# A ring of weight buffers that hands out the slot used longest ago, and lets two borrowed slots in at a channel mixer's first pair

## The chip, the cores and the metric

The kernel runs on one core of a Trainium2 chip. The metric is the device time of one execution in microseconds (us), lower is better. A core has five engines with an instruction queue each, which they work through in order: PE (matrix multiplication, with its weight loads listed as PEld), DVE (vector arithmetic), ACT (activations and copies with a scale), POOL and SP. In this kernel SP does nothing but issue DMA transfers, and POOL little else.

## The reference

A decoder trunk of two layers on 256 tokens of width 2048, in fp32. Each layer has a token mixer (gated linear attention in the first, forgetting attention in the second, both with cross-attention into 256 memory tokens) and then a channel mixer. What matters here is the passage from a token mixer's output projection into the channel mixer:

```python
x = x + gla_mixer(h, mk, mv, ...)        # ends in  concatenate([o, m]) @ w_out
h = rmsnorm(x, norm_ffn[i])
x = x + conv_ffn(h, ffn_w_up[i], ffn_conv_w[i], ffn_conv_b[i], ffn_w_down[i])

def conv_ffn(h, w_up, conv_w, conv_b, w_down):
    u = causal_dwconv(h @ w_up, conv_w, conv_b)      # 2048 -> 11264, causal convolution of width 3
    a, val = split_cols(u, [FFN_HIDDEN, FFN_HIDDEN])
    return (jax.nn.silu(a) * val) @ w_down           # 5632 -> 2048
```

## The kernel before

**Weights.** All weight matrices lie in one DRAM array `wp`, cut into units of 128 partitions x up to 1024 fp32 numbers (512 KB). Each unit is loaded by SP into a slot of a ring, the tile `raw`. Because fp32 products are made from two rounded parts, ACT copies the slot into `whi` (rounded), and DVE subtracts that copy from the slot into `wlo`. Each has five buffers. PE then multiplies activations that are split in the same way: whi with both activation parts, wlo with one, so that an ordinary unit of the projections shown here is 12 matmuls of 128x128 by 128x512. A slot is free again when its subtraction is done, a pair of whi and wlo buffers when PE is done with them. `split_unit` (load L232, copy L242, subtraction L243) does this for one unit.

**The ring.** Five slots lie in a tile of their own, `home`. During a channel mixer two more are added, halves of a tile `guest` (named raw2) that is allocated in a pool of that time. `raw_slot()` picks the slot of each load: a counter modulo the present length of the list. `ffn` appends the two guests when it begins and cuts the list back to five at its end.

**Pairs.** Most units of the mixers are worked by `pair_steps`. It takes a plan of the units of one panel; some neighbouring two of them form a pair, which is computed with seven block products (21 matmuls) in place of eight, by a scheme of Strassen's kind. Such a pair loads its two units at once (L440, into `ra` and `rb`), makes two copies and subtractions from them (`split_more`: L391, L392), then four subtractions in place (L446 to L449), and two further copies and subtractions. The first panel of a mixer is units 0 to 5 singly, then the pair (6, 7), then units 8 to 15. Its first pair multiplies sums of token blocks too (`usum`, made at L1460, L485 to L488, L696, L697).

**Into the channel mixer.** The output projection (`add_out`, its last panel at L347) produces 4 blocks of 512 columns. Each is added to x (L507), transposed by DVE into a tile `blk` (L1637), sent to DRAM (`far<-blk`, L659, on SP's queue), and later brought back turned (L664) and scaled and split into the activations' two parts (L551, L553). The returns of the last two blocks belong to the mixer's first panel: they are issued after units 2 and 9 and split after units 3 and 11. The tile `guest` is allocated once the pool that held `blk` has been closed, so its memory, and that of `usum`, can be that of `blk`.

**Order.** A scheduler orders the instructions of each engine's queue from the written order, priorities and its own estimate of times. Loads, copies and subtractions of weights have a priority 300 places ahead of where they are written. `tc.issue_after(i)` puts an instruction behind i on the same engine. The scheduler also adds every wait: the load into a slot waits for the last reader of that slot, or of what lay in that memory before.

Queues that matter: SP issues the unit loads, the transfers of the projection's blocks and the returns of blocks in the mixers' first panels; POOL issues the transfers inside the mixers.

Of the kernel before, what the change touches and what calls it, by code (L numbers as in the profile page):

```python
# [39 lines left out]
RAWS = 5  # L40
# [5 lines left out]
NUNIT = 1024  # L46
# [102 lines left out]
def _trunk(ctx: ExitStack, tc: tile.TileContext, xt, xtok, memt, wp, wgu, gns, gfin, cnv, par, msk, out):  # L149
# [36 lines left out]

    loads, casts, lows, ends, last_mm, sent = [], [], [], [], [], []
    home = rear.tile([P, RAWS * NUNIT], F32, name="raw")
    slots, taken = [home[:, i * NUNIT : (i + 1) * NUNIT] for i in range(RAWS)], [0]

    def raw_slot():

        taken[0] += 1
        return slots[taken[0] % len(slots)]
    scratch = [sm]
    parked = []

# [2 lines left out]
    def work(tag, bufs=1):  # L200
        return pwork.tile([P, 512], F32, name="ps_" + tag, tag=tag, bufs=bufs)
# [17 lines left out]
    def split_unit(unit, pieces=1, before=None, between=int):  # L219

        off, kcs, n = unit
        w = len(kcs) * n
        with tc.high_priority(offset=AHEAD):
            raw = raw_slot()
            hi = wpool.tile([P, NUNIT], F32R, name="whi", tag="whi", bufs=5)
            lo = wpool.tile([P, NUNIT], F32R, name="wlo", tag="wlo", bufs=5)
            src = wp[off : off + P * w].rearrange("(p n) -> p n", p=P)
            for i in range(pieces):
                s = slice(i * w // pieces, (i + 1) * w // pieces)
                if i:  # L230
                    between()
                loads.append(nc.sync.dma_start(raw[:, s], src[:, s]))  # L232
            if n % P:
                a, b, c = (t.rearrange("p (j m) -> p j m", j=len(kcs))[:, :, :n] for t in (raw[:, :w], hi, lo))
                casts.append(S.activation(b, a, AF.Copy))
                lows.append(V.tensor_tensor(c, a, b.bitcast(F32), ALU.subtract))
                return hi, lo
            for i in range(pieces):
                s = slice(i * w // pieces, (i + 1) * w // pieces)
                if before is not None:  # L240
                    before(i)
                casts.append(S.activation(hi[:, s], raw[:, s], AF.Copy))  # L242
                lows.append(V.tensor_tensor(lo[:, s], raw[:, s], hi[:, s].bitcast(F32), ALU.subtract))  # L243
        return hi, lo
# [141 lines left out]
    def split_more(src, n):  # L386

        with tc.high_priority(offset=AHEAD):
            hi = wpool.tile([P, NUNIT], F32R, name="whi", tag="whi", bufs=5)
            lo = wpool.tile([P, NUNIT], F32R, name="wlo", tag="wlo", bufs=5)  # L390
            casts.append(S.activation(hi[:, :n], src, AF.Copy))  # L391
            lows.append(V.tensor_tensor(lo[:, :n], src, hi[:, :n].bitcast(F32), ALU.subtract))  # L392
        return hi, lo

    def pair_steps(units, src, sums, flip, pool, early, late, ahead=0):

        bank = {}
        fast, slow = ("p1", "p5", "p7", "p6"), ("p2", "p3", "p4", "x")
        accs, works = (slow, fast) if flip else (fast, slow)
        tags = {n: ("acc", 4) for n in accs}  # L400
        tags.update(zip(works, (("o", 1), ("s", 2), ("s", 2), ("t", 1))))
        begun = set()
        sums = dict(sums)
        n = len(units)
        single = [k for k in range(n) if k not in sums and k - 1 not in sums]
        plan = []
        at = 0
        while at < n:
            if at + ahead in sums:
                plan.append(at + ahead)  # L410
                at += 2
            else:
                plan.append(single.pop(0))
                at += 1
        end = [k for k in plan if k in sums]

        def mm(name, x, w, last):
            if name not in bank:
                tag, bufs = tags[name]
                bank[name] = (pacc.tile([P, 512], F32, name="acc", tag="acc") if tag == "acc" else work(tag, bufs))  # L420
            r = TE.matmul(bank[name], x, w, start=name not in begun, stop=last)  # L421
            begun.add(name)
            return r

        def tok(k, b):
            return [src[k][:, part, b * P : (b + 1) * P] for part in range(2)]

        def three(name, x, w, last=False):
            for i, (a, b) in enumerate(((0, 0), (1, 0), (0, 1))):
                r = mm(name, x[a], w[b], last and i == 2)  # L430
            return r

        places = (("p2", 0, 0), ("p4", 1, 0), ("p3", 0, 1), ("x", 1, 1))
        for k in plan:
            if k in sums:
                with tc.high_priority(offset=AHEAD):
                    ra, rb = raw_slot(), raw_slot()
                    with tc.issue_after(loads[-1].ins):
                        for t, (off, _, w) in ((ra, units[k]), (rb, units[k + 1])):
                            loads.append(nc.sync.dma_start(t, wp[off : off + P * w].rearrange("(p n) -> p n", p=P)))  # L440
                st = [[sums[k][:, part, j, :] for part in range(2)] for j in (3, 0, 1, 2)]
                done = k == end[-1]
                w1 = split_more(ra[:, :512], 512)
                w2 = split_more(rb, 1024)
                with tc.high_priority(offset=AHEAD):
                    V.tensor_tensor(ra[:, :512], ra[:, 512:], ra[:, :512], ALU.subtract)  # L446
                    V.tensor_tensor(ra[:, 512:], rb[:, 512:], ra[:, 512:], ALU.subtract)  # L447
                    V.tensor_tensor(rb[:, 512:], rb[:, 512:], ra[:, :512], ALU.subtract)
                    summed = V.tensor_tensor(rb[:, :512], rb[:, :512], rb[:, 512:], ALU.subtract)  # L449
                three("p1", tok(k, 0), [t[:, :512] for t in w1], done)  # L450
                three("p2", tok(k + 1, 0), [t[:, :512] for t in w2])
                three("p3", st[3], [t[:, 512:] for t in w2])
                with tc.issue_after(summed.ins):
                    w3 = split_more(ra, 1024)
                three("p5", st[0], [t[:, :512] for t in w3], done)
                three("p7", st[2], [t[:, 512:] for t in w3], done)
                w4 = split_more(rb, 1024)
                three("p6", st[1], [t[:, 512:] for t in w4], done)
                last_mm.append(three("p4", tok(k + 1, 1), [t[:, :512] for t in w4]))
                if done:  # L460
                    with tc.issue_after(casts[-1].ins), tc.issue_after(lows[-1].ins):
                        early(bank)
                yield -1
                yield -1
                continue
            else:
                w = split_unit(units[k])
                last = k == n - 1
                steps = [(low, *place) for low in range(2) for place in places]
                if last:  # L470
                    steps.sort(key=lambda t: places.index(t[1:]))
                for low, name, b, h in steps:
                    for part in range(2 - low):
                        r = mm(name, tok(k, b)[part], w[low][:, h * 512 : (h + 1) * 512], last and low == 1)
                    if last and low:
                        ends.append(r)
                        late(b, h, bank[name])
                last_mm.append(r)
            yield k
# [923 lines left out]
    def ffn(l, nx, h, m, ys, zs, landing, then, pool, temps, last=None, spare=None):  # L1403
        with tc.tile_pool(name=f"ffn{l}", bufs=1) as fp:
# [3 lines left out]
            up_sums = {k: held("usum", k) for k in (*SEVEN_UP, SEVEN_MORE)}  # L1408
            rooms = {i: held("dsum", i) for i in range(2)}
            guest = pool.tile([P, 2 * NUNIT], F32, name="raw2")  # L1410
            slots.extend(guest[:, i * NUNIT : (i + 1) * NUNIT] for i in range(2))
            cw = fp.tile([P, 4 * 88], F32, name="cw")
            nc.sync.dma_start(cw, cnv[l])
            taps = [fp.tile([P, 2, 2, T + i], F32, name=f"tap{i}") for i in range(3)]
# [181 lines left out]
            else:  # L1596
                hooks = {(2, 3): then.land, (2, 5): then.land, (2, 7): then.take, (3, 1): then.take, (3, 2): then.land,
                         (3, 5): then.take}
                for f, step, at in ((2, f2, 3), (3, f3, 0)):
                    for u in range(at, 8):  # L1600
                        step(u)
                        hooks.get((f, u), int)()
            del slots[RAWS:]

    def preparing(name, dst, pool, far, kept=None, tag="blk", queue=nc.sync):

# [72 lines left out]
    with tc.tile_pool(name="store", bufs=1) as op:  # L1679
# [58 lines left out]
        then.begin, then.rooms = begin, None  # L1738
        more = [op.tile([P, 2, T], F32R, name=f"more{i}") for i in range(RING - KC)]
        ffn(1, n, bufA, bufB + more, ys, zs, zs, then, op, temps, last, spare)  # L1740


# [68 lines left out]
```

## Time and profile before

| | |
|---|---|
| time, median of 3 runs | 2221.41 us (2220.82 to 2221.58) |
| profiled execution, its own time | 2219.84 us |
| its span | 2218.0 us |
| busy: PE, PEld, DVE, ACT, POOL | 2196.9, 1846.7, 1828.6, 1437.8, 136.8 us |
| mean granted clock of PE | 0.997 |
| unit loads | 811 issues (741 of 512 KB, 70 smaller) |
| HBM read, written | 469.62 MB, 43.79 MB |

A row of a timeline has the start and the length in us, the engine, the line of the code, the operation, what it writes and reads, and how many instructions are merged in it; in brackets stands how long the engine had been idle and what ended that. A row of waits has who waited, for whom, the total in us, how many times, and the longest. A row of a table by stage has the stage, its length, the busy time (and number of instructions) of PE, PEld, DVE, ACT and POOL, the granted clock of PE, the share of the DMA engines and GB/s. Matmul lengths in a timeline overlap; the pace of PE is read from the starts. The first channel mixer begins at about 456 us of the span, the second at about 1493 us.

### The profile page before, as it was taken

What the parts mean: (1) busy time and instruction counts of PE and PEld (TensorE: products, weight loads), DVE (VectorE), ACT (ScalarE), POOL (GpSimd) and SP (SyncE); (2) the same over time, 40 slices, a digit from 0 to 9 for tenths busy, and PEclk for the clock granted to TensorE, in tenths of its full rate; (3) what the DMA queues carried; (4) which work ended last, traced back from release to release, by engine and by line L of the source; (5) the groups of instructions that cost most, each with busy time, mean ns of one, the idle gap of its engine ahead of it and who ended that gap; (6) DMA issues with size and microseconds to landing.
All of it is one profiled execution on the core that took longest, in us unless ns stands there. A gap on an engine that the chain in (4) does not pass through costs nothing.

```text
span 2218.0 us, 30190 instructions
## 1 busy us (share of the span) xinstructions
PE 2196.9 (99%) x10285; PEld 1846.7 (83%) x10285; DVE 1828.6 (82%) x2715; ACT 1437.8 (65%) x2280; POOL 136.8 (6%) x257
## 2 busy tenths in 40 slices
PE   9999999999999999999999999999999999999998
PEld 7888888878888888888888998877888888888886
DVE  7768976679988889889987569668998888988996
ACT  6655655557887568647865555445788657765874
POOL 0000000001100000001010000000100000100000
PEclk9999999999999999999999999999999999999999
DMA  9766666776777667666877667666687667776683
GB/s 360 260 222 217 199 207 230 252 231 223 258 250 239 199 228 256 231 207 224 268 246 245 219 207 235 224 217 223 224 263 248 222 203 245 242 236 211 230 283 113
DMA packets 166291, 515.41 MB, mean 232 GB/s; under 512 B 20780, under 2 KB 42552, under 8 KB 166136
## 3 DMA queue, kind: packets, MB, share of 16 engines
q1 hardware_dynamic: 149064, 460.99, 63.2%
q0 software_dynamic: 16496, 51.71, 7.4%
q8 instruction: 80, 1.31, 0.2%
q10 hardware_dynamic: 576, 0.79, 0.1%
q14 instruction: 75, 0.61, 0.1%
HBM read 469.62 MB, written 43.79 MB: 231 GB/s over the span
## 4 chain that ended last, share of the span: by engine, by line
PE 96%; DVE 2%; ACT 1%; DMA 1%; issue 0%; SPq 0%; DVEq 0%; ACTq 0%
PE acc L421 29%; PE acc L347 26%; PE ps_s L421 15%; PE ps_o L421 7%; PE ps_t L421 7%; PE acc L273 3%; PE acc L318 3%; PE ps_s L347 2%; PE acc L377 2%; PE acc L271 1%; PE ps_s L1044 0%; DMA raw<-wp 0%; ACT whi L242 0%; PE ps_o L710 0%; PE ps_s L710 0%
## 5 line engine op out<-in xcount | busy, mean ns | idle before, releaser
L243 DVE TENSOR_TENSOR wlo<-raw,whi 128x1024 fp32r<-128x1024 f32 (+2 forms) x685 | 812.5, 1200 | 222.9 <-ACT whi L242 200.8
L242 ACT ACTIVATE whi<-raw 128x1024 fp32r<-128x1024 f32 (+2 forms) x685 | 704.3, 1045 | 347.8 <-PE acc L347 131.2
L347 PE MATMUL acc<-whi,B 128*128 128x512 f32 (+3 forms) x1248 | 290.9, 369 | 0.0
L391 ACT ACTIVATE whi<-raw 128x1024 fp32r<-128x1024 f32 (+1 forms) x184 | 173.7, 953 | 179.4 <-DVE raw L447 65.7
L347 PEld LDWEIGHTS acc<-whi,B 128*128 128x128 f32 x1248 | 226.8, 188 | 28.1
L392 DVE TENSOR_TENSOR wlo<-raw,whi 128x1024 fp32r<-128x1024 f32 (+1 forms) x184 | 198.3, 1084 | 26.8 <-ACT whi L391 23.8
L421 PE MATMUL acc<-whi,mix 128*128 128x512 f32 x746 | 191.7, 392 | 8.7 <-ACT whi L242 8.7
L421 PE MATMUL acc<-whi,B 128*128 128x512 f32 x720 | 186.9, 389 | 0.0
L421 PEld LDWEIGHTS acc<-whi,mix 128*128 128x128 f32 x746 | 141.2, 189 | 38.7 <-ACT whi L242 9.2
L347 PE MATMUL acc<-wlo,B 128*128 128x512 f32 (+3 forms) x624 | 159.1, 369 | 0.0
L421 PEld LDWEIGHTS acc<-whi,B 128*128 128x128 f32 x720 | 135.1, 188 | 28.5 <-ACT whi L242 0.5
L347 PEld LDWEIGHTS acc<-wlo,B 128*128 128x128 f32 x624 | 114.2, 188 | 14.6
L1425 ACT ACTIVATE tap<-yzu,cw 128x256 f32<-128x256 f32 x264 | 120.7, 534 | 5.4 <-DMA yzu<-far 5.4
L1425 ACT ACTIVATE tap<-fvt,cw 128x256 f32<-128x256 f32 x264 | 120.2, 530 | 3.1 <-DMA fvt<-far 3.1
L1432 DVE TENSOR_TENSOR tap<-tap,tap 128x1024 f32<-128x1024 f32 x88 | 106.7, 1213 | 9.0 <-ACT tap L1425 9.0
L421 PE MATMUL acc<-wlo,mix 128*128 128x512 f32 x373 | 105.0, 392 | 0.0
L421 PE MATMUL acc<-wlo,B 128*128 128x512 f32 x360 | 103.8, 389 | 0.0
L421 PE MATMUL ps_s<-whi,mix 128*128 128x512 f32 x374 | 103.8, 389 | 0.0
L421 PE MATMUL ps_s<-whi,B 128*128 128x512 f32 x324 | 89.9, 389 | 0.0
L421 PEld LDWEIGHTS acc<-wlo,mix 128*128 128x128 f32 x373 | 70.6, 189 | 14.8
L421 PEld LDWEIGHTS ps_s<-whi,mix 128*128 128x128 f32 x374 | 70.2, 188 | 14.6
L421 PEld LDWEIGHTS acc<-wlo,B 128*128 128x128 f32 x360 | 67.6, 188 | 14.0
(503 smaller groups left out, 3912.8 us busy)
## 6 DMA issues: line engine op xcount, KB each, us to landing
raw<-wp SPq DMA_DIRECT2D x741, 512.0 KB, 4.6
fvt<-far POOLq DMA_DIRECT2D x100, 128.0 KB, 5.2
raw<-wp SPq DMA_DIRECT2D x32, 384.0 KB, 3.4
far<-yu POOLq DMA_DIRECT2D x22, 512.0 KB, 3.0
far<-yzu POOLq DMA_DIRECT2D x22, 512.0 KB, 3.0
yzu<-far POOLq DMA_DIRECT2D x88, 128.0 KB, 4.8
raw<-wp SPq DMA_DIRECT2D x24, 388.0 KB, 3.5
x<-xtok SPq DMA_DIRECT2D x8, 512.0 KB, 7.0
```

Source lines behind the costliest of these rows:

```text
L242: casts.append(S.activation(hi[:, s], raw[:, s], AF.Copy))
L243: lows.append(V.tensor_tensor(lo[:, s], raw[:, s], hi[:, s].bitcast(F32), ALU.subtract))
L271: mm = TE.matmul(acc[p][c][:, :T], w[:, s], both[:, 0, :], start=False, stop=end and j == 3)
L273: mm = TE.matmul(acc[p][c], w[:, s], both, start=u == j == 0, stop=end and j == 3)
L318: mm = TE.matmul(acc[b][:, :n], src[kcs[j] - base][:, part, b * P : (b + 1) * P], w, start=u == 0 and low == part == j == 0, stop=u == end ...
L347: mm = TE.matmul(acc[b][:, :n], src[kc - base][:, part, b * P : (b + 1) * P], ready[low][:, j * room : j * room + n], start=i == low == pa ...
L377: mm = TE.matmul(acc[b][:, :n], src[kc - base][:, part, b * P : (b + 1) * P], w, start=i == low == part == j == 0, stop=i == end and low = ...
L391: casts.append(S.activation(hi[:, :n], src, AF.Copy))
L392: lows.append(V.tensor_tensor(lo[:, :n], src, hi[:, :n].bitcast(F32), ALU.subtract))
L421: r = TE.matmul(bank[name], x, w, start=name not in begun, stop=last)
L1425: S.activation(by_run(taps[i][:, s, c, i:]), zs[slot][:, :, 2 * c + s], AF.Copy if i else AF.Identity, bias=0.0 if i else w[3], scale=w[2 ...
L1432: V.tensor_tensor(taps[0], taps[0], taps[n][:, :, :, :T], ALU.add)
```

## The change

`raw_slot` now rotates the list: the slot at the front, the one handed out longest ago, goes to the back and is handed out. `ffn` no longer appends its two guests at once; it keeps them in `coming`, and the next `pair_steps` pair puts them at the front of the list just before it takes its two slots. At the end of `ffn` the guests are filtered out of the list wherever they stand.

```diff
-    slots, taken = [home[:, i * NUNIT : (i + 1) * NUNIT] for i in range(RAWS)], [0]
+    slots, coming = [home[:, i * NUNIT : (i + 1) * NUNIT] for i in range(RAWS)], []
 
     def raw_slot():
 
-        taken[0] += 1
-        return slots[taken[0] % len(slots)]
+        slots.append(slots.pop(0))
+        return slots[-1]
...
             if k in sums:
                 with tc.high_priority(offset=AHEAD):
+                    slots[:0] = coming
+                    del coming[:]
                     ra, rb = raw_slot(), raw_slot()
...
             guest = pool.tile([P, 2 * NUNIT], F32, name="raw2")
-            slots.extend(guest[:, i * NUNIT : (i + 1) * NUNIT] for i in range(2))
+            guests = [guest[:, i * NUNIT : (i + 1) * NUNIT] for i in range(2)]
+            coming.extend(guests)
...
-            del slots[RAWS:]
+            slots[:] = [s for s in slots if not any(s is g for g in guests)]
```

## Prediction

> **What bounds the kernel now.** First the page: span, the chain that ended last, then who made PE wait.
>
> ```profile
> span 2218.0 us, 30190 instructions
> ...
> PE 96%; DVE 2%; ACT 1%; DMA 1%; issue 0%; SPq 0%; DVEq 0%; ACTq 0%
> ```
>
> ```profile
> PE acc L421 <- ACT whi L242: 8.7, 1, 8.7
> PE ps_o L185 <- DVE B L182: 1.5, 1, 1.5
> PE ps_t L421 <- ACT whi L391: 0.9, 1, 0.9
> ```
>
> PE carries 96% of the chain, so a change pays only where it shortens a PE stall. The waits of PE name one large stall, 8.7 us, and two small ones; the 1.5 us is the start of the program. PE's timeline puts the large one at the first unit of the second channel mixer (L421 is its matmul, L347 that of the output projection ahead of it):
>
> ```profile
> 1488.06 1.98 PE L347 MATMUL acc<-whi,B 128*128 128x512 f32 x8
> 1489.87 1.07 PE L347 MATMUL acc<-wlo,B 128*128 128x512 f32 x4
> ...
> 1493.04 0.61 PE L347 MATMUL acc<-wlo,B 128*128 128x512 f32 x2
> 1502.39 3.78 PE L421 MATMUL acc<-whi,mix 128*128 128x512 f32 x8 [8.73 <-ACT whi L242]
> ...
> 1510.46 1.75 PE L421 MATMUL acc<-whi,mix 128*128 128x512 f32 x7
> ```
>
> Eight matmuls start 1489.87 - 1488.06 = 1.81 us apart: 0.2268 us each, the undisturbed rate, 2.72 us for a unit of 12. The last two of the projection start at 1493.04, so the next could start at 1493.49; it starts at 1502.39, 8.90 us late. The 24 matmuls of units 0 and 1 then take 1510.46 - 1502.39 = 8.07 us and not 24 x 0.2268 = 5.44: 2.63 us more. The table by stage says why:
>
> ```profile
> 1498.00:1502.00 4.00, 0.00 (x0) 0.00 (x0) 0.69 (x1) 1.18 (x2) 0.00 (x0) 0.50 0.74 261
> 1502.35:1510.40 8.05, 8.01 (x24) 6.38 (x25) 8.03 (x14) 6.97 (x10) 0.00 (x0) 0.67 0.65 196
> 1510.40:1520.00 9.60, 9.60 (x44) 7.93 (x44) 7.81 (x10) 3.18 (x3) 0.00 (x0) 1.00 0.89 247
> ```
>
> The granted clock (third column from the end) falls to 0.50 in the idle stretch, is 0.67 over the two units and 1.00 after them. The stall costs 8.90 + 2.63 = 11.53 us. What it waited for is in the chain of that window:
>
> ```profile
> 1495.16 2.57 DMA far<-blk
> ...
> 1497.78 3.42 DMA raw<-wp
> ...
> 1501.28 1.06 ACT whi L242
> ```
>
> The load of unit 0 could not be issued until the normalised input's last block (blk) had been read out to DRAM: the slot it goes to is a guest slot, and its memory was blk's.
>
> **The ring, by counting calls.** From the loops of the code, 160 slots are taken before the first mixer, 264 in it, 120 between the mixers, 264 in the second. The old rule takes the counter modulo the length, so at a change of length it jumps. First mixer: unit 0 gets the slot of the load just before it; units 1 to 4 the slots of six loads before; unit 5 guest a, unit 6 guest b, unit 7 slot 0. Second mixer: unit 0 gets guest b; units 1 to 5 the slots of six before; unit 6 guest a, unit 7 guest b again. The new rule gives units 0 to 5 slots used five loads before, and units 6 and 7, the first pair, the two guests. From the pair on the distance is seven under both, and after the first mixer five (seven for one load). So only the first eight loads of each mixer differ; all loads, copies and matmuls remain in number and size.
>
> **Second mixer, units 0 to 5.** The release of a slot is the end of the subtraction (wlo, L243) that last read it:
>
> ```profile
> 1469.41 1.22 DVE L243 TENSOR_TENSOR wlo<-raw,whi 128x1024 fp32r<-128x1024 f32 x1 [1.50 <-ACT whi L242]
> 1470.66 0.35 SPq L232 DMA_DIRECT2D raw<-wp  x1
> ...
> 1482.39 0.85 SPq L232 DMA_DIRECT2D raw<-wp  x2
> 1495.16 0.33 SPq L659 DMA_DIRECT2D far<-blk  x1
> 1497.78 0.33 SPq L232 DMA_DIRECT2D raw<-wp  x1
> 1498.16 0.42 SPq L440 DMA_DIRECT2D raw<-wp  x1
> 1493.12 0.42 ACT L635 ACTIVATE sq<-x 128x256 f32<-128x256 f32 x1 [11.27 <-DVE x L507]
> ```
>
> The slot of five loads before unit 0 (unit 3 of the projection's last panel) is free at 1469.41 + 1.22 = 1470.63; before, unit 1's load took it at 1470.66. Now unit 0 goes there, 27 us earlier than 1497.78, and units 1 to 4 take the places of units 2 to 5, the last by 1482.39 + 0.85. They were landing that early already, but ACT, which works in order, sat idle 11.27 us behind unit 0's copy. That copy can now run at about 1482, when the projection's unit 3 gives back its whi buffer, against a need at 1493.49. Unit 5 reuses unit 0's slot and is needed five units later. This removes 11.53 us.
>
> **The first pair is late next.** Both its loads wait for blk's transfer (before, the one at L440, 1498.16, did, and the other waited for unit 0's guest). Behind them on SP's queue may stand units 8 to 11 and the return of the last block (L664); ACT's copy of usum shares the same memory. When blk leaves here is not in the trace, since PE stood still. The nearest rows are the first mixer's, where PE ran through:
>
> ```profile
> 456.60:482.10 25.50, 24.55 (x106) 19.48 (x106) 17.21 (x27) 12.75 (x22) 0.00 (x0) 1.00 0.70 217
> ```
>
> ```profile
> 456.66 1.07 PE L421 MATMUL acc<-whi,B 128*128 128x512 f32 x4
> ...
> 477.50 0.73 PE L421 MATMUL ps_t<-whi,usum 128*128 128x512 f32 x2 [0.92 <-ACT whi L391]
> ...
> 482.16 1.98 PE L421 MATMUL acc<-whi,B 128*128 128x512 f32 x8
> ```
>
> ```profile
> 461.23 0.33 SPq L659 DMA_DIRECT2D far<-blk  x1
> 465.97 0.33 SPq L232 DMA_DIRECT2D raw<-wp  x1
> 466.35 0.90 SPq L440 DMA_DIRECT2D raw<-wp  x2
> ```
>
> ```profile
> 469.33 1.06 ACT L242 ACTIVATE whi<-raw 128x1024 fp32r<-128x1024 f32 x1 [2.65 <-DMA raw<-wp]
> 470.69 0.63 ACT L391 ACTIVATE whi<-raw 128x512 fp32r<-128x512 f32 x1 [0.30 <-DMA raw<-wp]
> 472.46 1.07 ACT L391 ACTIVATE whi<-raw 128x1024 fp32r<-128x1024 f32 x1 [1.13 <-DMA raw<-wp]
> ...
> 476.38 1.06 ACT L391 ACTIVATE whi<-raw 128x1024 fp32r<-128x1024 f32 x1 [1.52 <-DVE raw L449]
> ```
>
> There blk left 461.23 - 456.66 = 4.57 us after unit 0 began and was away 465.97 - 461.23 = 4.74 us later; then three guest-bound loads (unit 5, unit 6, unit 7) landed at about 469.33, 470.69, 472.46. With unit 5 out of the queue the pair lands one place earlier: 469.33 and 470.69. From unit 7's landing to the end of the pair's last copy took 476.38 + 1.06 - 472.46 = 4.98 us, so that copy would end at 475.67. PE, unhindered, has 72 matmuls of units 0 to 5 and 15 of the pair ahead of its use: 456.66 + 87 x 0.2268 = 476.39. Slack 0.7 us. In the second mixer the same offsets from 1493.49 give the same 0.7 us: hidden, barely. I bound the pair's new stall per mixer between 0 and the 1.69 us that the first mixer loses now (next), and take 0.15 us each, since the computed slack is positive but smaller than a landing varies.
>
> The blk transfer took 2.57 us in the idle machine at 1495.16 and 4.74 us at 461.23 amid loads; I used the longer. The Trainium skill, "DMA: Bandwidth & Descriptors", section "Latency and other measured facts", says the receipt of a write to HBM is slower under load; the two rows agree in direction.
>
> **First mixer.** The 106 matmuls of that window include one already running, so 105 started between 456.66 and 482.16: 25.50 us against 105 x 0.2268 = 23.81, a loss of 1.69 us, 0.92 of it at the pair's last operand. Now unit 5 has an ordinary slot (unit 0's, read by about 448) and the pair lands earlier, as above. It gains 1.69 at most and, with the copies in the same order and the same late release, 0 at least. Unit 0's load also stops waiting for the load just before it; that hit no PE wait, so it counts nothing.
>
> **Sum.** 11.53 + 1.69 - 2 x 0.15 = 12.9 us. Elsewhere PE has no wait to lose or win; the return to five slots costs nothing, as that load is only looser. The profiled execution's own time is 2219.84 us (span 2218.0), 1.57 below the median 2221.41: 2221.41 - 12.9 = 2208.5.
>
> On the clock: the Trainium skill, "TensorE: Matmul & The Clock Gate", Part 1, gives half clock after an idle window of about 3.4 us, lifted after about 3.4 us of work. Half a rate lost over 3.4 us would be an estimate of 1.7 us for my 2.63, and 2209.4 in all; the trace has the low clock longer, so the rows stand.
>
> **Rivals.** (a) The pair takes over the wait. For: slack of 0.7 us in a chain of transpose, transfer, load, two copies and four subtractions. Against: the same chain met the first mixer's pace nearly. If blk leaves 2 us later (SP's in-order queue holding one more load, that of unit 12, ahead of it), each mixer's pair stalls about 1.3 us: 2208.2 + 2.6 = 2210.8. With 3 us each, 2214. (b) The first mixer gains nothing: 2221.41 - 11.53 + 0.15 = 2210.0. (c) Within 0.2% (4.4 us, about what this kernel's measurement can tell): the order is computed anew by the scheduler, and if it again puts a guest-bound item, such as ACT's usum copy, ahead of unit 0's copy, PE stalls as before: about 2221. For: in the second mixer usum's copy did stand ahead of it. Against: in the first it stands behind unit 4's. (d) Slower: the pair in the second mixer waits so long that more than the 11.53 us comes back. Its place is SP's queue at the guest loads; it decides when they issue over 13 us later than 1493.49 + 9.31 = 1502.8, past 1516, and 4.4 us more to be told, that is past 1520. Only a load that waits for late work, put ahead of blk's transfer, could do that; the longest candidates I see are 2 us.
>
> **Chances.** Forecast, 2206 to 2210: 0.62. (a) and (b), up to 2214: 0.24. Between that and (c): 0.05. (c) 0.05. (d) 0.04. Faster 0.90, within 0.2% 0.06, slower 0.04. The range is 2206 (the full 13.2 us and 2 us of run-to-run) to 2213.
>
> **What would show it.** In the second mixer: PE without a wait at the first unit, clock 1.00 through it, the unit loads at L232 before blk's far transfer, both loads at L440 right after it. In the first: L440's two loads follow blk's transfer with no L232 between, and ps_t's 0.92 us gone. The prediction is wrong if a PE wait of over 2 us appears at a first pair, or if waits appear far from both places.

## The result, and the profile after

The changed kernel takes 2210.43 us (median of 5 runs, 2208.67 to 2210.61) against 2221.41 us before (5 runs, 2219.92 to 2224.24): a ratio of 0.9948, 95% interval 0.9935 to 0.9962, so 11.0 us less. The profiled execution of the new kernel has its median time, 2210.43 us; the one of before stands 1.57 us under its median. Between the two profiles there are therefore only 9.4 us, and it is those that the accounts below divide up. Lines of the code after the change are 2 or 3 higher than before (L440 is L442, L659 is L661).

The head of the page and the waits of PE, after:

```profile
span 2208.6 us, 30197 instructions
...
PE 95%; DVE 2%; DMA 1%; ACT 1%; issue 0%; SPq 0%; DVEq 0%; ACTq 0%
```

```profile
PE ps_t L421 <- ACT whi L391: 2.0, 4, 1.2
PE ps_o L185 <- DVE B L182: 1.5, 1, 1.5
PE acc L347 <- ACT whi L242: 0.3, 1, 0.3
```

The 8.7 us at the second mixer's first unit are gone, and `ps_t` of the pairs has risen from 0.9 us in one wait to 2.0 us in four: 0.29 and 1.18 us at the two first pairs, and 0.23 and 0.26 us at the first pairs of the two second panels (569.88 and 1607.51 us). PE's timeline at that first unit (L347 is the projection, L421 the mixer):

```profile
1492.99 0.62 PE L347 MATMUL acc<-wlo,B 128*128 128x512 f32 x2
1493.44 1.07 PE L421 MATMUL acc<-whi,mix 128*128 128x512 f32 x4
...
1514.07 0.73 PE L421 MATMUL ps_t<-whi,usum 128*128 128x512 f32 x2 [1.18 <-ACT whi L391]
```

Unit 0 follows 0.45 us after the last two matmuls of the projection started, that is without a gap; 1.18 us are waited 20 us later, at the first pair. The table by stage (columns as before the change; the granted clock is third from the end):

```profile
1498.00:1502.00 4.00, 4.00 (x19) 3.34 (x18) 0.01 (x1) 1.06 (x1) 0.00 (x0) 1.00 0.73 242
1502.35:1510.40 8.05, 8.05 (x37) 6.69 (x36) 4.27 (x7) 2.57 (x4) 0.00 (x0) 1.00 0.75 236
1510.40:1520.00 9.60, 8.42 (x37) 6.60 (x37) 9.48 (x14) 7.75 (x12) 0.00 (x0) 1.00 0.57 164
```

Where the clock stood at 0.50 and 0.67 it is now 1.00, and the 8.05 us that held 24 matmuls hold 37. The stage after them is the one that has got worse: PE is idle for 9.60 - 8.42 = 1.18 us of it. SP's timeline there:

```profile
1480.92 16.79 SPq L232 DMA_DIRECT2D raw<-wp  x7
1498.01 0.33 SPq L661 DMA_DIRECT2D far<-blk  x1
1503.34 0.84 SPq L442 DMA_DIRECT2D raw<-wp  x2
1504.23 0.43 SPq L666 DMA_DIRECT2D yzu<-far  x1
```

The single units' loads (L232) now stand ahead of blk's transfer; the pair's two (L442) directly behind it. The chain of work that ended last, around the pair:

```profile
1497.36 0.63 DVE blk L1640
...
1498.01 5.31 DMA far<-blk
...
1503.34 0.33 SPq L442
...
1503.71 5.30 DMA raw<-wp
...
1509.10 1.07 ACT whi L391
...
1510.19 1.24 DVE wlo L392
...
1512.96 1.07 ACT whi L391
...
1514.07 0.73 PE ps_t L421 x2
```

It is the predicted chain, transfer, load, copy, subtractions, last copy, and it ends at 1512.96 + 1.07 = 1514.03, with PE waiting. In the first mixer the same chain is nearly in time; SP's timeline, and PE's:

```profile
461.27 0.33 SPq L661 DMA_DIRECT2D far<-blk  x1
466.08 0.81 SPq L442 DMA_DIRECT2D raw<-wp  x2
```

```profile
476.42 0.74 PE L421 MATMUL ps_t<-whi,usum 128*128 128x512 f32 x2 [0.29 <-ACT whi L391]
```

No load at L232 stands between the two any more, and the wait of 0.92 us there has become 0.29.

**A ledger.** Every trace has 10285 matmuls. Setting the start of the n-th of one, from the beginning of its span, against the n-th of the other shows where time is gained (negative) or lost, in us against the profile of before; "end" is the difference at the last matmul, which is that of the spans:

| kernel | first mixer, first pair | first mixer, second panel | second mixer, entry | second mixer, first pair | second mixer, second panel | elsewhere | end |
|---|---|---|---|---|---|---|---|
| after | -1.07 | +0.99 | -11.52 | +1.52 | +0.60 | 0.0 | -9.5 |
| after, repeated (e9) | -1.03 | +0.93 | -11.52 | +1.13 | +0.63 | +0.4 | -9.4 |
| e1 | +0.94 | 0 | -11.52 | +2.16 | -0.35 | +0.1 | -8.7 |
| e2 | -1.27 | +1.25 | -11.52 | +0.34 | +0.57 | +0.4 | -10.3 |
| e3 | +0.71 | 0 | -11.52 | 0 | -0.35 | +0.4 | -10.8 |
| e4 | -1.16 | +0.98 | -11.52 | 0 | -0.35 | +1.4 | -10.6 |
| e5 | -1.70 | 0 | -11.52 | 0 | -0.35 | +0.4 | -13.2 |
| e5, repeated (e11) | -1.70 | 0 | -11.52 | 0 | -0.29 | -0.6 | -14.1 |
| e6 | -0.15 | 0 | -11.52 | +1.63 | +0.49 | +1.8 | -7.8 |
| e7 | -1.70 | +0.84 | -11.52 | 0 | +1.39 | +4.8 | -6.2 |
| e8 | -1.70 | 0 | -11.52 | 0 | -0.35 | -0.3 | -13.9 |
| e10 | -1.39 | +0.24 | -11.52 | +0.03 | 0 | -0.5 | -13.2 |

The second panel is the stretch some 90 to 120 us after a mixer's beginning (about 550 to 570 and 1590 to 1616 us). Of "elsewhere", -0.6 to +0.9 us arise in the first 456 us, ahead of both mixers: profiles of single executions differ by about that much where PE's and SP's queues are the same.

### The profile page after: what moved, and what is told of

The parts are those of the page before. It is cut to its first block, busy times and chain, and to the rows that moved or that the text cites. A ratio compares the mean times of both kernels' runs of the same rounds, so it can differ in the third digit from the quotient of the medians.

```text
span 2208.6 us, 30197 instructions
## 1 busy us (share of the span) xinstructions
PE 2195.5 (99%) x10285; PEld 1845.1 (84%) x10285; DVE 1828.1 (83%) x2715; ACT 1435.6 (65%) x2280; POOL 136.8 (6%) x257
## 4 chain that ended last, share of the span: by engine, by line
PE 95%; DVE 2%; DMA 1%; ACT 1%; issue 0%; SPq 0%; DVEq 0%; ACTq 0%
PE acc L421 27%; PE acc L347 26%; PE ps_s L421 15%; PE ps_o L421 7%; PE ps_t L421 7%; PE acc L318 3%; PE acc L273 3%; PE ps_s L347 2%; PE acc L377 2%; PE acc L271 1%; ACT whi L391 0%; DMA raw<-wp 0%; DMA far<-blk 0%; DVE wlo L392 0%; PE ps_s L1046 0%
## 5 line engine op out<-in xcount | busy, mean ns | idle before, releaser
L243 DVE TENSOR_TENSOR wlo<-raw,whi 128x1024 fp32r<-128x1024 f32 (+2 forms) x685 | 815.3, 1205 | 211.7 <-ACT whi L242 194.6
L347 PE MATMUL acc<-whi,B 128*128 128x512 f32 (+3 forms) x1248 | 290.8, 369 | 0.0
L347 PEld LDWEIGHTS acc<-whi,B 128*128 128x128 f32 x1248 | 226.8, 188 | 28.1
L421 PE MATMUL acc<-whi,mix 128*128 128x512 f32 x746 | 191.3, 389 | 0.0
L421 PE MATMUL acc<-whi,B 128*128 128x512 f32 x720 | 187.4, 389 | 0.0
L421 PEld LDWEIGHTS acc<-whi,mix 128*128 128x128 f32 x746 | 140.0, 188 | 29.2
L347 PE MATMUL acc<-wlo,B 128*128 128x512 f32 (+3 forms) x624 | 159.1, 369 | 0.0
L421 PEld LDWEIGHTS acc<-whi,B 128*128 128x128 f32 x720 | 135.1, 188 | 28.3
L347 PEld LDWEIGHTS acc<-wlo,B 128*128 128x128 f32 x624 | 114.2, 188 | 14.6
L1435 DVE TENSOR_TENSOR tap<-tap,tap 128x1024 f32<-128x1024 f32 x88 | 107.1, 1217 | 14.2 <-ACT tap L1428 13.9
L421 PE MATMUL acc<-wlo,mix 128*128 128x512 f32 x373 | 105.2, 389 | 0.0
L421 PE MATMUL acc<-wlo,B 128*128 128x512 f32 x360 | 104.0, 389 | 0.0
L421 PE MATMUL ps_s<-whi,mix 128*128 128x512 f32 x374 | 103.8, 389 | 0.0
L421 PE MATMUL ps_s<-whi,B 128*128 128x512 f32 x324 | 89.9, 389 | 0.0
L421 PEld LDWEIGHTS ps_s<-whi,mix 128*128 128x128 f32 x374 | 70.2, 188 | 14.6
L421 PEld LDWEIGHTS acc<-wlo,mix 128*128 128x128 f32 x373 | 70.0, 188 | 14.5
L421 PEld LDWEIGHTS acc<-wlo,B 128*128 128x128 f32 x360 | 67.6, 188 | 14.0
```

Source lines behind the costliest of these rows:

```text
L347: mm = TE.matmul(acc[b][:, :n], src[kc - base][:, part, b * P : (b + 1) * P], ready[low][:, j * room : j * room + n], start=i == low == pa ...
L1435: V.tensor_tensor(taps[0], taps[0], taps[n][:, :, :, :T], ALU.add)
```

## Experiments

Each is an edit to the kernel after the change unless the text says before. The letters of theories are those that the expectations use: A is the account on which the prediction rests. Medians stand beside those of the kernel before that ran on the same chip.

**e1: join at the start, with the new rule.** The guests go to the back of the list when the mixer begins.

```diff
-            coming.extend(guests)
+            slots.extend(guests)
```

> The slot used longest ago is given, but the two guests are appended when the mixer begins, at the back of the ring, so that unit 5 and the first half of the pair get them in both mixers. Theory A (what costs is a guest slot used before the projection's pool is handed over, after the last block's transfer): the second mixer's 11.5 us at unit 0 are gone; the first mixer is as in the kernel before (1.7 us lost up to unit 9), and the second loses 1.5 to 3.5 us at unit 5 and the pair, since three guest-bound or later loads follow the transfer. Time 2212 to 2213. Rival B (the jump of the counter at the change of length cost, not the guests): no jump is left here, so the time is that of the changed kernel, 2210.4, and no PE wait appears at unit 5.

Measured 2211.14 us (2210.86 to 2211.48) against 2220.44, ratio 0.9958 [0.9944, 0.9973]. Its waits of PE:

```profile
PE ps_t L421 <- ACT whi L391: 2.5, 2, 1.3
...
PE acc L421 <- ACT whi L242: 0.6, 1, 0.6
```

The entry is gained whole without any late joining: five home slots go to units 0 to 4, so unit 0 gets no guest. What joining late adds is at the pair, where the ledger loses 0.94 and 2.16 us here. The total came about 1 us under theory A's and 0.7 us over its rival's. The places are A's: the 0.6 us at `acc` is unit 5 of the first mixer, where the rival had no wait. That the first mixer would be as before was a miss, since it loses 0.94 us more. The kernel after is ahead of e1 by 0.7 us by medians, or by 1.7 us if each is set against the kernel before that ran with it; it is no more than that because e1 is without the second panels' losses (ledger).

**e2: join at the first pair, with the old counter** (an edit to the kernel before).

```diff
+                    slots.extend(coming)
+                    del coming[:]
                     ra, rb = raw_slot(), raw_slot()
...
-            slots.extend(guest[:, i * NUNIT : (i + 1) * NUNIT] for i in range(2))
+            guests = [guest[:, i * NUNIT : (i + 1) * NUNIT] for i in range(2)]
+            coming.extend(guests)
```

> The old counter modulo the ring's length, with the jump at the change of length, but the guests join at the first pair. In the second mixer the pair gets both guests, as in the changed kernel; in the first mixer guest b goes to the pair's second half and guest a to unit 12. Theory A: time within 1 us of the changed kernel (2209.5 to 2211.5), the second mixer alike to 0.3 us. Rival B: the jump returns, so a good part of the 11 us does: 2215 or more.

Measured 2209.83 us (2209.25 to 2210.8) against 2220.44, ratio 0.9953 [0.9937, 0.997]. It is the kernel after, within what can be told. That the second mixer would be alike to 0.3 us was a miss: the pair loses 0.34 us here and 1.52 us after, though DVE's and SP's queues have the same order there. What differs is how long the same transfer took, 4.76 us here:

```profile
1498.42 0.33 SPq L662 DMA_DIRECT2D far<-blk  x1
1503.18 0.80 SPq L443 DMA_DIRECT2D raw<-wp  x2
```

So either half of the change by itself removes the 11.52 us, since either keeps a guest from unit 0; beside the late joining the rule of the slot used longest ago brings nothing measurable.

**e3 and e4: a tile of its own for the second mixer's guests**, in a pool opened ahead of the pool that holds `blk`; e3 is the kernel before with it, e4 the kernel after.

```diff
-            guest = pool.tile([P, 2 * NUNIT], F32, name="raw2")
+            guest = own if l else pool.tile([P, 2 * NUNIT], F32, name="raw2")
...
+    ring2 = ctx.enter_context(tc.tile_pool(name="ring2", bufs=1))
+    own = ring2.tile([P, 2 * NUNIT], F32, name="raw2")
     with tc.tile_pool(name="turn2", bufs=1) as tp:
```

> The kernel before with its counter and with guest b at unit 0 of the second mixer, but the second mixer's guests lie in a pool of their own, opened before the pool that holds the projection's blocks. Theory A: the load of unit 0 no longer waits for the last block's transfer and is issued over 20 us earlier; PE's 8.7 us wait and the low clock behind it vanish, 11.5 us in all: 2209 to 2211. The pair does not wait either. The first mixer stays as before (1.7 us lost). Rival B: the wait at unit 0 stays, 2221.

> The changed kernel with the second mixer's guests in a pool of their own, opened before the pool of the projection's blocks. Theory A: the second mixer's first pair loses the 1.3 us it has now (PE's 1.2 us wait at ps_t), the rest as the changed kernel: 2208.5 to 2209.5. A rival, that the pair's 1.3 us come from the work of the pair itself (copies and subtractions in a row on ACT and DVE, delayed by evacuations) and not from the late loads: they stay, 2210.4.

e3 measured 2209.62 us (2208.5 to 2210.72) against 2220.44, ratio 0.9952 [0.9937, 0.9966]; e4 2208.03 us (2207.99 to 2209.24), ratio 0.9946 [0.9931, 0.9961]. SP's and PE's timelines of e3, where unit 0 still takes a guest, as in the kernel before:

```profile
1481.57 1.43 SPq L232 DMA_DIRECT2D raw<-wp  x2
1483.04 3.17 SPq L440 DMA_DIRECT2D raw<-wp  x2
1488.09 10.79 SPq L232 DMA_DIRECT2D raw<-wp  x4
1499.17 0.33 SPq L659 DMA_DIRECT2D far<-blk  x1
```

```profile
1494.15 0.62 PE L347 MATMUL acc<-wlo,B 128*128 128x512 f32 x2
1494.60 1.07 PE L421 MATMUL acc<-whi,mix 128*128 128x512 f32 x4
```

All these loads, the pair's at L440 included, leave before blk does, and unit 0 follows the projection without a gap. The order of slots of before does no harm where the guest is free; the wait came from the memory alone. In e4 the 1.52 us at the second mixer's pair are gone too, which puts them down to the guests' wait for blk; its time came just below the range expected. In e3 the first mixer, whose queues on PE and SP are those of before, loses 0.71 us more than before: a pair that is late anyway varies by that much.

**e5: join one panel later.** No guest before the second panel, in both mixers.

```diff
-            coming.extend(guests)
...
                 first(k)
+            coming.extend(guests)
             done = 4
```

> The changed kernel with the guests let in one panel later: the first panel, its pair too, works on the five slots, and the guests join at the first pair of the second panel. Theory A (the pair's remaining stalls come from guest-bound loads behind the last block's transfer): the pair's loads are issued before that transfer in both mixers, PE's waits at its ps_t go (1.2 and 0.3 us; 1.3 and 0.6 us of lost pace): 2208.0 to 2209.5. Rival: seven slots are needed from the first pair on, and five make the units after it late: 2212 or more.

Measured 2206.14 us (2205.59 to 2207.08) against 2221.42, ratio 0.9932 [0.9918, 0.9946]: below the range expected. SP's timeline in the second mixer, and the stage of the first pair:

```profile
1485.65 3.05 SPq L442 DMA_DIRECT2D raw<-wp  x2
1491.09 5.36 SPq L232 DMA_DIRECT2D raw<-wp  x2
1496.74 0.33 SPq L661 DMA_DIRECT2D far<-blk  x1
```

```profile
1510.40:1520.00 9.60, 9.60 (x44) 7.97 (x43) 9.60 (x22) 7.11 (x10) 0.00 (x0) 1.00 0.89 317
```

With five slots the pair's loads leave 11 us before blk, and PE has no idle time in the stage where the kernel after has 1.18 us. The first mixer gains its 1.70 us whole. The second panels' losses are gone as well, which was not expected.

**e6: join at unit 3**, which puts a guest earlier than at the pair.

```diff
             else:
+                if k == 3:
+                    slots[:0] = coming
+                    del coming[:]
                 w = split_unit(units[k])
```

> The changed kernel with the guests let in earlier, at unit 3, so that units 3 and 4 of each mixer's first panel get them. A dose: theory A says that a guest-bound load is issued 9.4 us after unit 0 begins in the first mixer and 7 to 10 us in the second, is landed 3.4 to 5.7 us later and copied 1.06 us after that, while unit 3 is needed 8.2 us after unit 0. So PE waits 5.6 to 6 us in the first mixer and 3 to 8 us in the second, and up to 2.6 us more each where the clock falls: 2219 to 2228. Rival B (slot distances alone matter; here they are as regular as in the changed kernel): 2210.4.

Measured 2210.66 us (2209.68 to 2212.09) against 2221.42, ratio 0.9951 [0.9935, 0.9967]: a miss. SP's timeline in both mixers:

```profile
459.25 0.33 SPq L664 DMA_DIRECT2D far<-blk  x1
461.84 0.81 SPq L232 DMA_DIRECT2D raw<-wp  x2
...
1496.58 0.33 SPq L664 DMA_DIRECT2D far<-blk  x1
1499.17 0.80 SPq L232 DMA_DIRECT2D raw<-wp  x2
```

The guests' loads still wait for blk, but blk leaves 1.67 us after unit 0 (457.58 and 1494.92 here) and not 4.57, and its transfer takes 2.59 us and not 4.74 to 5.31. So the loads go out some 5 us earlier than I had reckoned in the first mixer, and unit 3 waits 0.7 us in each mixer. The offset that the prediction took from one row of before isn't a constant: in this kernel's order DVE works the split of the block ahead of blk (L558, which is L555 in the kernel after) at 467.73 us, behind blk's transposes; in the kernel after it does so in front of them.

**e7: no guests at all**, five slots throughout.

```diff
-            coming.extend(guests)
```

> The guests are allocated but never join: five slots throughout, given in turn. If the two extra slots are worth something beyond the first panel, PE waits appear at pairs or three units after them in every panel (46 pairs, 0.3 to 1 us each: 2222 to 2255). If five slots are enough for this pace (a pair's slots are free about 12 us after their loads are issued, and PE has 8 us of single units behind a pair), the time is that of the kernel with the late join, 2208 to 2212.

Measured 2213.65 us (2212.49 to 2214.71) against 2221.42, ratio 0.9966 [0.9953, 0.9979], between the two expectations. The guests are worth 2213.65 - 2206.14 = 7.5 us to e5. Nothing is lost at the first pairs. One stage late in the second mixer costs 3.51 us:

```profile
2085.00:2095.00 10.00, 10.00 (x45) 8.27 (x45) 7.09 (x11) 8.47 (x16) 0.76 (x2) 1.00 0.95 311
2095.00:2105.00 10.00, 8.42 (x29) 6.11 (x28) 9.52 (x12) 7.47 (x9) 0.00 (x0) 0.83 0.40 135
```

A pair's operand comes 1.34 us late there, the granted clock is 0.83 on average, and 29 matmuls fit where 45 did.

**e8: both cures**, late joining in the first mixer and a pool of its own in the second.

```diff
-            coming.extend(guests)
+            if l:
+                coming.extend(guests)
...
+            if not l:
+                coming.extend(guests)
             done = 4
```

> The late join (second panel) in the first mixer, and a pool of their own with the join at the first pair in the second. Theory A: no guest-bound load is late in either mixer; 2207.5 to 2209, within 1 us of the kernel with the late join in both.

Measured 2206.03 us (2205.7 to 2206.55) against 2221.42, ratio 0.9932 [0.9919, 0.9945]: below the range expected, and the same as e5. Two different ways of not waiting for blk come to the same time.

**e9 to e11, on one chip:** the kernel after once more, the kernel after with the split of the block ahead of blk asked for two units later, and e5 once more. The edit of e10:

```diff
-                {2: lambda: nx.land(landing[0]), 3: nx.take, 8: nx.col,
+                {2: lambda: nx.land(landing[0]), 5: nx.take, 8: nx.col,
```

> The changed kernel once more, for its spread and beside the next two. If the 1.3 us lost at the second mixer's first pair come of the way DMA work happens to land (the last block's transfer took 5.3 us, and the pair's second load 5.3 us), this profile shows another loss there, between 0.3 and 2 us; if they are fixed by the order of the queues, 1.2 to 1.4 us again. Time 2209 to 2211.5.

> The changed kernel, but the split of the block before the last (eight DVE operations of 0.27 us at L555, that stand in DVE's queue ahead of the last block's transposes) is written after unit 5 and not after unit 3. Theory C (the pair's loads are late because the last block reaches its transfer late, behind other DVE work): the transfer leaves 2 to 2.5 us earlier in both mixers, the pair's loads with it, and the PE waits at ps_t of the first pairs go: 1.3 and 0.6 us, 2208 to 2209. Rival D (the wait is the pair's own chain of copies and subtractions): they stay.

> The kernel whose guests join at the second panel's first pair, once more, on the same chip as the changed kernel: 2205.5 to 2207, 3 to 5 us below it.

Against 2220.82 us: e9 2210.22 (2209.29 to 2210.57), ratio 0.995 [0.9937, 0.9962]; e10 2206.85 (2206.64 to 2209.83), ratio 0.994 [0.9927, 0.9952]; e11 2206.18 (2205.78 to 2206.98), ratio 0.9934 [0.992, 0.9947]. e9 and e11 came within their ranges, e10 below its own. Two of the five executions of e10, at 2209.05 and 2209.83 us, lie where the kernel after does; the profile is that of the fastest, and no profile shows what those two lost. DVE's timeline at the end of the projection, first in the kernel after, then in e10:

```profile
1492.25 1.14 DVE L555 SCALAR_TENSOR_TENSOR mix<-yzu,gains,mix 128x128 fp32r<-128x128 f32 x4
1493.30 0.68 DVE L509 TENSOR_TENSOR x<-x,acc 128x512 f32<-128x512 f32 x1
1493.90 1.14 DVE L555 SCALAR_TENSOR_TENSOR mix<-yzu,gains,mix 128x128 fp32r<-128x128 f32 x4
...
1496.18 1.19 DVE L243 TENSOR_TENSOR wlo<-raw,whi 128x1024 fp32r<-128x1024 f32 x1
1497.28 0.70 DVE L1640 STREAM_TRANSPOSE blk<-x 128x512 f32<-128x512 f32 x1
```

```profile
1490.68 0.69 DVE L509 TENSOR_TENSOR x<-x,acc 128x512 f32<-128x512 f32 x1
...
1492.76 0.71 DVE L1640 STREAM_TRANSPOSE blk<-x 128x512 f32<-128x512 f32 x1
```

In the kernel after, the last addition to x and the transposes that make blk queue behind eight instructions of L555, in two groups of 1.14 us, and the last transpose behind a weight subtraction (L243) too, which in e10 comes after it. Without these, the last transpose ends at 1492.76 + 0.71 = 1493.47 and not 1497.98, and SP's timeline of e10 has the transfer out 4.5 us earlier, and the pair's loads 6.7 us earlier:

```profile
1493.50 0.33 SPq L661 DMA_DIRECT2D far<-blk  x1
1494.61 0.33 SPq L232 DMA_DIRECT2D raw<-wp  x1
1496.62 0.80 SPq L442 DMA_DIRECT2D raw<-wp  x2
```

About 1.6 us of either is PE itself being ahead (unit 0 begins at 1491.84 in e10, at 1493.44 after). The other 2.2 us between 4.5 and 6.7 are the transfer, which takes 1496.62 - 1493.50 = 3.12 us here. With blk leaving 1493.50 - 1491.84 = 1.66 us after unit 0 the pair loses 0.03 us, though it takes the same two guests as in the kernel after and they still wait for blk. The profile bears theory C out: blk was late because of DVE's order.

The fastest is e5, run twice; on the last chip it is 2210.22 - 2206.18 = 4.0 us ahead of the kernel after, and the ranges of the two do not touch. It beats both kernels.

## Why the prediction was right, and where a term was off

The forecast was 2208.5 us, 2206 to 2213; measured 2210.43, so faster, in the range, 1.9 us above the value. Between the two profiles, whose rows the forecast added up, the gain is 9.4 us and not 12.9: two terms were misjudged, by 3.5 us together. That the time came only 1.9 us off is in part luck, since the profile of before stands 1.57 us under its median and that of after does not.

- **Units 0 to 5 of the second mixer: right to the hundredth.** 11.53 us worked out, 11.52 in the ledger of every variant that keeps unit 0 off a guest that waits. Adding the half-clock units to the stall was needed for that: the wait alone is 8.9. ACT's timeline has unit 0's copy where it was expected, at about 1482:

```profile
1481.85 1.06 ACT L242 ACTIVATE whi<-raw 128x1024 fp32r<-128x1024 f32 x1
```

- **"Its memory was blk's": the wait was right, the reason too narrow.** In the plan of the memory of the compiled kernel before, the second mixer's guest doesn't overlap the last blk: in each partition it lies at bytes 160256 to 168448, blk at 139776 to 143872. The pool that held blk is handed over to the next pool as a whole, and what is allocated in its place waits for the last reader in it. e3 shows that a tile from another pool doesn't wait; the rest of this is read from the plan, and no run separates it.
- **The pair, "hidden, barely": the mis-sized term.** 0.15 us each were taken; the second mixer lost 1.52, and the first kept 0.62 of its 1.69. blk left at 1498.01 - 1493.44 = 4.57 us after unit 0, exactly the offset used. Then the transfer took 5.31 us and not 4.74, and the second load landed 1509.01 - 1503.34 = 5.67 us after the first was issued and not 470.69 - 465.97 = 4.72: together 0.57 + 0.95 = 1.52 us late. The copies and subtractions took 1514.03 - 1509.01 = 5.02 us, where 4.98 were reckoned. The slack against this was smaller than worked out: not 87 matmuls stand ahead of the late operand but 85, in the first mixer of before, from which the forecast was made, and in both mixers after. That leaves 456.66 + 85 x 0.2268 = 475.94 against 475.67, or 0.27 us and not 0.7. In the second mixer the operand was needed at 1493.44 + 85 x 0.2268 = 1512.72 and its first matmul began at 1514.07, 1.35 us late; that is most of the ledger's 1.52 us, which equals the lateness of the landings by chance (the trace's wait of 1.18 us counts from the end of the matmul ahead). A slack smaller than the spread of two transfers in a row was counted as if it held. The same kernel run again lost 1.13, and e2, with the same loads in the same order, 0.34, so the size of it varies from run to run.
- **"Elsewhere PE has no wait to lose": wrong.** The second panels lost 0.99 and 0.60 us, 90 us and more after the pair. Waits far from both places were among the prediction's own signs of being wrong, so on this point it was, small as the waits are (0.23 and 0.26 us). The waits of ACT in the first mixer's second panel, after and then before:

```profile
ACT tap L1441 <- DVE tap L1435: 6.2, 1, 6.2
```

```profile
ACT tap L1438 <- DVE tap L1432: 1.2, 1, 1.2
```

ACT stands 6.2 us behind one DVE addition of the convolution; weight copies come after it in ACT's queue. In the second mixer it is 5.7 us after and 0.7 before. Wherever that wait is 5.7 us or more (the kernel after, both times, e2, and e4's first mixer) the second panel loses 0.57 to 1.25 us; wherever it is 1.4 or less it loses 0.49 at most, except in e7, with five slots (0.84 and 1.39). The two go together over the runs, which is not a test: no run changed this order by itself, so whether it is the cause, and why the scheduler writes that order, stay open.
- **The sum.** 11.52 + 1.07 - 1.52 - 0.99 - 0.60 = 9.48.
- **The rivals.** (a) came about in part: its 2210.8 is nearer to the result than the forecast's value, though through slower landings and a smaller slack, not a later blk. (b) had 2210.0, as near, and the first mixer did end with next to nothing, but by gaining 1.07 at the pair and giving 0.99 back a panel later. (c) and (d) didn't occur; the scheduler put unit 0's copy where it was needed.

## What to carry to other kernels

A buffer that is allocated at the start of a stage is free only when the last work in the memory handed over is done; find the first load that goes to it and ask who needs that load. Let such buffers join a ring after the stage's last late transfer (e5), or allocate them in a pool opened earlier (e8 in its second mixer): here that took off 15 us, where changing which load gets them took off 11. When a stall is taken away, reckon the next user of the same late event with the slowest landings in the trace, and look at what queues ahead of that event's producer: moving some other work on DVE two units later (e10) brought, by medians, 3.4 of the 4.0 us that e5 brought, though not in every execution.

## What the runs showed of the hardware

The transfer of the same block took 2.6 us where the last unit load had been issued over 5 us ahead of it (before, second mixer: 2.57; e6: 2.59), 3.1 us with 2.7 us between them (e10), and 4.6 to 5.4 us wherever a unit load had gone out 0.6 us ahead of it (before, first mixer: 4.74; after, second: 5.31). The Trainium skill, "DMA: Bandwidth & Descriptors", section "Latency and other measured facts", has access to HBM slower at high load; the direction agrees, and the runs do not separate that from waiting behind the loads' own bytes.

A wait of 1.18 us left the granted clock at 1.00 (after), 8.73 us took it to 0.50 (before), and there it stayed at 0.50 for the first 5.3 us of work, to 1507.7 us, half of which is about the 2.63 us lost. In e7 the clock was 0.50 for 3.4 us, from 2099.7 to 2103.1, beginning 1.8 us after a wait of 1.34 us had ended. The Trainium skill, "TensorE: Matmul & The Clock Gate", Part 1, lets the clock fall after an idle window of about 3.4 us: the first two agree with it, e7's does not as it stands, and no run here says why.
